# A hybrid two-layer backbone on one core: an earlier modulation vector, a rotation on VectorE, and a pinned VectorE order

## The chip, the cores and the metric

One core of a Trainium2 chip runs the whole program. The metric is the device time of one execution in microseconds (us); where several runs were made, their median.

## The reference

The program is a two-layer backbone over 512 latent tokens and 256 context tokens with a model width of 1024, all in fp32. Every sub-block reads a normalised and modulated copy of the stream, `rms(x) * (1 + scale) + shift`, and adds its result back times a gate. Shift, scale and gate are vectors of width 1024 per layer; there are six of them (modulations 0 to 5), each the product of a conditioning vector with a 1024 x 1024 block of a weight matrix, once for the latent and once for the context tokens.

- Layer 0: a convolution module and a bidirectional mLSTM side by side; their outputs together (width 1024) go through an out-projection, times gate 2, into the stream. Then a convolutional feed-forward network (FFN).
- Layer 1: multi-head latent attention, 16 heads. Queries come from a 512-wide latent, keys and values from a 256-wide one. Each head has 64 plain and 32 rotary components; both are normalised over the 96 (QK-norm), and the rotary part is turned by a position-dependent angle, which is two products and a sum. The attended values go through an out-projection, times gate 2, into the stream. Then a second FFN.

```python
def _modulate(x, shift, scale):
    return _rms(x) * (1 + scale) + shift
```

## The kernel before, in words

The stream lies in SBUF as eight tiles `xr`, one for each block of 128 features (index m or k), 128 partitions by 768 tokens: latent first (`LSEG`), then context (`CSEG`); `HSEG` are the two latent halves of 256 tokens. A product in fp32 is made of three matmuls, high by high, low by high and high by low part. `weights` (L158) brings a weight tile: a DMA on SP's queue into `wr`, a rounding copy `wh` on ScalarE (L113), and the difference `wl` on the engine that `lo_eng` names (L167), VectorE or, in some stages, GpSimd (POOL). `residual` adds gate times projection to the stream on VectorE (`xr<-pab,mods,xr`, or `pmo` in the attention, L119); `sumsq` squares the new stream tile on ScalarE (`sq`) and adds it into `ss` on POOL or VectorE (L253), after k; `norm_rows` sums `ss` over partitions on TensorE (`pr`) and takes the reciprocal root in eleven small VectorE instructions (`ra`, `rs`, then three rounds of `rz`, `rz`, `rs`; L199 ff.); `pb` spreads the result over the partitions by TensorE; then `u`, `fh`, `fl` make the modulated stream in two parts.

A scheduler orders the instructions of each engine by priority and by when they become ready in its own model; each engine then runs its list in order. Three places matter here.

- **Out-projection of layer 0** (`mixer0`, L533, its last loop over m, L716 ff.; 400 to 465 us). For each of the first six m, 48 matmuls `pab` over 768 tokens; m = 6 and 7 go by segment. A background generator `ada_gemv` (L335) makes modulation 5 meanwhile, in two halves of 512 columns. A half is eight loads `gr` (256 KB each on SP's queue, two buffers) with two VectorE instructions each that add row block times conditioning value into the accumulators `ga` (one for latent, one for context); `ada_sum` (L357) then folds the partitions by eight pairs of small matmuls `pac<-selv,ga` on TensorE, called the fold-in below, and VectorE puts the result into `mods`. At the end of each m, `self.step(AOS)` (L724) runs AOS steps of the generator; AOS is a constant at L44.
- **First queries of the attention** (`mixer1`, call at L1227; `prep_q`, L1286). After the queries' reciprocal root `rq`, the engine given as last argument scales the query tile `qt` (128 x 1536, L1301) and rotates its rotary part with eight smaller instructions (L1309 to L1312). Around it VectorE copies the low parts of the values `v`, makes a `wl`, and runs the keys' chain: `ssk`, `ra`, `rk`, `rz` ..., and `kt` (L1362, L1363), which TensorE's transposes `ptr` (L1378) wait for.
- **Last attention projection** (`project(3)`, L1446). All eight m for the first latent half, then for the second; before m = 4 of the second (`NRM`), the norm of the first half is issued (`norm_rows(HSEG[0])`). The FFN that follows begins with that norm's `pb`.

Of the kernel before, what the change touches and what calls it, by code (L numbers as in the profile page):

```python
# [19 lines left out]
LAT = 512  # L20
CTX = 256
T = LAT + CTX
# [7 lines left out]
HSEG = ((0, LAT // 2, 0), (LAT // 2, LAT, 0))  # L30
# [10 lines left out]
GRID_W = 64  # L41
NEG = -1.0e30
WPRIO = 300
AOS = 5  # L44
SLB = 6
PADB = 6
TAP = 8
# [33 lines left out]
class Net:  # L81
# [97 lines left out]
    def proj_tok(self, ps, wt, w0, wn, xs, t, nk, first=True, last=True, k0=0):  # L179
        wh, wl = wt  # L180
        for k in range(nk):
            xh, xl = xs[k0 + k]
            for j, (w, x) in enumerate(((wh, xh), (wl, xh), (wh, xl))):
                self.mm(ps, x[:, t * P:(t + 1) * P], w[:, k, w0:w0 + wn],
                        first and k == 0 and j == 0, last and k == nk - 1 and j == 2)

    def ahead(self, gen, prio):

        while True:
            with self.tc.high_priority(offset=prio):  # L190
                if next(gen, self) is self:
                    return
            yield
# [339 lines left out]
    def mixer0(self, pes):  # L533
# [3 lines left out]
        with ExitStack() as es:  # L537
# [178 lines left out]
            for m in range(KD - KDL):  # L716
# [5 lines left out]
                for seg in both:  # L722
                    self.sumsq(xs[m], m, seg, ob, "sq", bufs=2)
                self.step(AOS)  # L724
            ws = {m: self.weights(wout, 0, KD, m * P, P) for m in range(KD - KDL, KD)}
# [426 lines left out]
    def mixer1(self, xs):  # L1152
        nc, tc, d = self.nc, self.tc, self.d
        win = d["mla_w_in"][0]
        wuq, wukv, wout = d["mla_w_uq"][0], d["mla_w_ukv"][0], d["mla_w_out"][0]
        with ExitStack() as es:
# [8 lines left out]
            with ExitStack() as hes:  # L1165
# [5 lines left out]
                def tmp(s):  # L1171
                    return tp.tile([P, T], F32, tag="t", name=self.name(s))
# [52 lines left out]
                    nc.vector.tensor_scalar(kvt[t][:, :256], kvt[t][:, :256], rk[:, t:t + 1], None, op0=ALU.mult)  # L1225
                qt0 = self.query_tile(ap)
                for _ in self.prep_q(0, qt0, cqs, tb, wuq, lambda: tmp("sq")[:, :4 * QK].rearrange("p (h c) -> p h c", c=QK),  # L1227
                                     [xs[k][:, LAT:T] for k in (2, 3)], nc.gpsimd):
                    pass
                for k in range(2):  # L1230
                    ps = self.psum("pkvT")
# [82 lines left out]
    def attention(self, es, ap, qt0, xs, cqs, kvs, krr, ssr, tb, wuq, wukv, wout):  # L1314
        nc, tc = self.nc, self.tc
        tk = es.enter_context(tc.tile_pool(name="tk", bufs=1))
        qts, kts, vts, heads, prob, pts, outs, ohl, sums = {}, {}, {}, {}, {}, {}, {}, {}, {}
# [97 lines left out]
        def values(i):  # L1415
            h, u = divmod(i, 2)
            pr, hh = divmod(h, 2)
            pt = pts.pop(i)
            v = vts[pr]
            pv = self.pt("T", "ppv")  # L1420
            for j in range(NT):
                for p, x in enumerate(pt[j // 2]):
                    self.mm(pv[:, :256], v[:, j, hh, :], x[:, j % 2, :], j == 0 and p == 0, j == NT - 1 and p == 1)
            o = xs[4 + (2 * pr + u) % 4][:, LAT:T]
            outs[pr, u] = o
            own = slice(64 * hh, 64 * hh + 64)
            oth = slice(64 - 64 * hh, 128 - 64 * hh)
            tmp = xs[i % 2][:, LAT:T]
            self.act(tmp[own], pv[oth, :256])
            self.tt(o[own], pv[own, :256], tmp[own], ALU.add)  # L1430
            if i % 4 == 3:
                oh = tk.tile([P, LAT], F32R, tag="oh", bufs=2, name=self.name("oh"))
                ol = tk.tile([P, LAT], F32R, tag="ol", bufs=2, name=self.name("ol"))
                r = share.pop(pr)
                ps = self.pt("T", "pshr")
                for t in range(NTL):
                    self.mm(ps[:, t * P:(t + 1) * P], self.sel_two(t), r, True, True)
                for u in range(2):
                    c = slice(u * 256, (u + 1) * 256)
                    self.tt(outs[pr, u], outs[pr, u], ps[:, c], ALU.mult)  # L1440
                    self.split(outs[pr, u], oh[:, c], ol[:, c])
                ohl[pr] = (oh, ol)
                if pr % 2:
                    self.bg.append(project(pr // 2))

        def project(g):  # L1446
            ins = [ohl[2 * g], ohl[2 * g + 1]]
            if g == 3:
                ws = [self.weights(wout, 2 * g, 2, m * P, 512) for m in (0, 4)]
                for seg in HSEG:  # L1450
                    for m in range(KD):
                        if seg is HSEG[1] and m == NRM:
                            self.norm_rows(HSEG[0])
                        ps = self.pt("T", "pmo")
                        self.proj(ps, ws[m // 4], (m % 4) * P, ins, 2, (seg,))
                        self.residual(xs[m], ps, 1, 2, m, (seg,))
                        self.sumsq(xs[m], m, seg, tk, "pe", bufs=4)
                    yield
                return
            for m in range(0, KD, 4):  # L1460
                w = self.weights(wout, 2 * g, 2, m * P, 512)
                for i in range(4):
                    ps = self.pt("T", "pmo")
                    self.proj(ps, w, i * P, ins, 2, (LSEG,))
                    self.residual(xs[m + i], ps, 1, 2, m + i, (LSEG,))
                    yield
# [119 lines left out]
```

## Time and profile before

| | |
|---|---|
| time, median of 3 runs | 1783.05 us (1782.91, 1783.05, 1785.39) |
| profiled execution, its time | 1782.59 us |
| span of its trace | 1780.8 us |
| mean granted TensorE clock | 0.96 of full |
| busy: TensorE (PE), weight loads | 94 %, 85 % |
| busy: VectorE (DVE), ScalarE (ACT), POOL | 63 %, 38 %, 14 % |
| DMA | 95 GB/s mean |

A `timeline` row gives start, duration, engine, line, operation, output<-inputs by name, shapes, how many instructions the row joins (x), and in brackets the idle time ahead of it with what ended that. TensorE's own rows of a chain are matmuls at line 110. A granted clock of 1.00 stands for 2.4 GHz and 0.50 for 1.2 GHz.

### The profile page before, as it was taken

To read this page: it belongs to the slowest core of one execution; us is meant where nothing else is said; L and a number is where in the kernel's file an instruction comes from. 1 tells how busy PE (TensorE), PEld (TensorE's weight loads), DVE (VectorE), ACT (ScalarE), POOL (GpSimd) and SP (SyncE) were. 2 spreads that over 40 slices of the span, in tenths; PEclk is the share of its full clock that TensorE was granted. 3 is DMA by queue.
4 is the path that set the end of the run, shared out by engine and by line. 5 is a ranking of instruction groups with operands and counts; after the bars stand their busy time and mean duration, and the time that the engine had idled before them with its cause. 6 is when DMAs were issued, how large, how long until landed. Compare 5 with 4: busy or idle time off the path is not lost.

```text
span 1780.8 us, 24171 instructions
## 1 busy us (share of the span) xinstructions
PE 1679.1 (94%) x9436; PEld 1519.1 (85%) x9436; DVE 1130.3 (63%) x1743; ACT 679.2 (38%) x1364; POOL 246.0 (14%) x331
## 2 busy tenths in 40 slices
PE   6998698769999999999999998999999799999999
PEld 3998476659899999999999878999988788888887
DVE  3799964745876555474334487777788854444544
ACT  4421042542331221212222346777876442332232
POOL 2342132425100000000000111223140200000000
PEclk8999799779999999999999999999999899999999
DMA  9621442233253345262221332001110133333332
GB/s 311 216 61 42 135 143 83 61 118 100 74 159 106 108 142 166 84 200 67 64 60 49 97 96 61 32 13 36 44 35 25 36 95 97 101 98 95 95 95 83
DMA packets 194747, 168.43 MB, mean 95 GB/s; under 512 B 8552, under 2 KB 168214, under 8 KB 194632
## 3 DMA queue, kind: packets, MB, share of 16 engines
q1 hardware_dynamic: 191936, 163.30, 29.8%
q0 software_dynamic: 1280, 3.35, 0.8%
q8 instruction: 75, 1.23, 0.3%
q10 hardware_dynamic: 1416, 0.21, 0.1%
q14 instruction: 40, 0.33, 0.1%
HBM read 161.55 MB, written 5.29 MB: 94 GB/s over the span
## 4 chain that ended last, share of the span: by engine, by line
PE 81%; DVE 10%; DMA 3%; ACT 3%; issue 1%; POOL 1%; SPq 0%; ACTq 0%; DVEq 0%; POOLq 0%
PE pfo L110 17%; PE pfg L110 16%; PE pfv L110 16%; DVE acc L593 6%; PE psc L110 4%; PE pab L110 3%; PE ppv L110 2%; PE pt L1409 2%; PE po L110 2%; PE pf L110 2%; PE pmo L110 2%; PE puq L110 2%; PE pukv L110 2%; PE pv L110 1%; PE pn L110 1%
## 5 line engine op out<-in xcount | busy, mean ns | idle before, releaser
L113 ACT ACTIVATE wh<-wr 128x1024 fp32r<-128x1024 f32 (+3 forms) x205 | 204.4, 999 | 625.0 <-PE pfo L110 215.5
L167 DVE TENSOR_TENSOR wl<-wr,wh 128x1024 fp32r<-128x1024 f32 (+3 forms) x171 | 195.8, 1147 | 194.4 <-ACT wh L113 190.5
L110 PE MATMUL pfo<-hh,wh 128*128 128x384 f32 (+2 forms) x528 | 166.8, 355 | 0.0
L110 PE MATMUL pfo<-hl,wh 128*128 128x384 f32 (+2 forms) x528 | 166.6, 355 | 0.0
L110 PE MATMUL pfo<-hh,wl 128*128 128x384 f32 (+2 forms) x528 | 166.2, 354 | 0.0
L110 PE MATMUL pfg<-fh,wh 128*128 128x384 f32 (+1 forms) x504 | 152.0, 355 | 0.0
L110 PE MATMUL pfg<-fl,wh 128*128 128x384 f32 (+1 forms) x504 | 151.6, 354 | 0.0
L110 PE MATMUL pfg<-fh,wl 128*128 128x384 f32 (+1 forms) x504 | 151.2, 354 | 0.0
L110 PE MATMUL pfv<-fh,wl 128*128 128x384 f32 (+1 forms) x504 | 150.8, 353 | 0.0
L110 PE MATMUL pfv<-fl,wh 128*128 128x384 f32 (+1 forms) x504 | 150.8, 353 | 0.0
L110 PE MATMUL pfv<-fh,wh 128*128 128x384 f32 (+1 forms) x504 | 150.7, 353 | 0.0
L119 DVE SCALAR_TENSOR_TENSOR xr<-pfo,mods,xr 128x512 f32<-128x512 f32 (+1 forms) x128 | 83.7, 665 | 104.4 <-PE pfo L110 103.8
L593 DVE SCALAR_TENSOR_TENSOR acc<-up,par,acc 128x783 f32<-128x783 f32 x120 | 146.9, 1249 | 4.4 <-ACT acc L113 2.3
L167 POOL TENSOR_TENSOR wl<-wr,wh 128x1024 fp32r<-128x1024 f32 (+1 forms) x34 | 85.3, 2512 | 296.9 <-ACT wh L113 280.2
L253 POOL TENSOR_TENSOR ss<-ss,sq 128x256 f32<-128x256 f32 (+1 forms) x31 | 32.1, 1044 | 573.5 <-ACT sq L113 572.6
L119 DVE SCALAR_TENSOR_TENSOR ga<-gr,cc,ga 128x1024 f32<-128x1024 f32 (+1 forms) x84 | 96.0, 1161 | 22.6 <-DMA gr<-in_ada_w_dram 22.3
L110 PEld LDWEIGHTS pfo<-hl,wh 128*128 128x128 f32 x528 | 98.1, 189 | 8.9 <-issue 0.2
L110 PEld LDWEIGHTS pfo<-hh,wh 128*128 128x128 f32 x528 | 97.9, 189 | 9.0 <-ACT hh L113 0.4
L110 PEld LDWEIGHTS pfo<-hh,wl 128*128 128x128 f32 x528 | 97.9, 189 | 8.7
L116 DVE TENSOR_TENSOR ft<-ft,pfv 128x768 f32<-128x768 f32 (+1 forms) x42 | 34.4, 820 | 109.9 <-PE pfv L110 109.9
L110 PEld LDWEIGHTS pfg<-fh,wh 128*128 128x128 f32 x504 | 92.8, 189 | 6.5
L110 PEld LDWEIGHTS pfg<-fl,wh 128*128 128x128 f32 x504 | 92.8, 189 | 6.4
(418 smaller groups left out, 3711.0 us busy)
## 6 DMA issues: line engine op xcount, KB each, us to landing
wr<-in_ffn_w_in_dram SPq DMA_DIRECT2D x88, 512.0 KB, 4.0
gr<-in_ada_w_dram SPq DMA_DIRECT2D x48, 512.0 KB, 4.5
wa<-in_ada_w_dram SPq DMA_DIRECT2D x20, 1024.0 KB, 8.1
wr<-in_ffn_w_out_dram SPq DMA_DIRECT2D x32, 512.0 KB, 3.5
wr<-in_ab_w_in_dram SPq DMA_DIRECT2D x20, 512.0 KB, 5.2
wr<-in_ffn_w_out_dram SPq DMA_DIRECT2D x24, 384.0 KB, 3.3
gr<-in_ada_w_dram SPq DMA_DIRECT2D x16, 256.0 KB, 2.7
wr<-in_mla_w_out_dram SPq DMA_DIRECT2D x8, 512.0 KB, 3.4
```

What stands on the lines that cost most here:

```text
L110: self.nc.tensor.matmul(out, lhsT=lhsT, rhs=rhs, start=start, stop=stop)
L113: self.nc.scalar.activation(out, in_, func, **kw)
L116: self.nc.vector.tensor_tensor(out, a, b, op=op)
L119: self.nc.vector.scalar_tensor_tensor(out, a, s, b, op0=op0, op1=op1, **kw)
L167: self.lo_eng.tensor_tensor(lo[:, :n], raw[:, :n], hi[:, :n].bitcast(F32), op=ALU.subtract)
L253: eng.tensor_tensor(self.ss[:, s:e], self.ss[:, s:e], sq[:, s:e], op=ALU.add)
L593: nc.vector.scalar_tensor_tensor(acc[:, :CONVO], up[:, k:k + CONVO], self.convw[:, 4 * k + ct:4 * k + ct + 1], acc[:, :CONVO], op0=ALU.mul ...
L1409: nc.tensor.transpose(pt[:, o:o + P], pe[:, (j + jj) * P:(j + jj + 1) * P], self.ident)
```

## The change

Three edits. A: AOS is 9 instead of 5, so each m of the out-projection of layer 0 carries nine steps of the modulation generator. B: the first queries are scaled and rotated by VectorE instead of POOL. C: the VectorE instructions traced from the norm of the first half to the end of the second half's projection are tied to the order in which the program emits them.

```diff
@@ -41,7 +41,7 @@
-AOS = 5
+AOS = 9
@@ -183,6 +183,19 @@
+    def traced(self):
+        return self.nc.cur_bb.bb.instructions
+
+    def in_order(self, start, engine):
+
+        last = None
+        for i in list(self.traced())[start:]:
+            if i.engine == engine:
+                if last is not None:
+                    info = mybir.DependencyInfo(mybir.DependencyClass.NoSync, mybir.DependencyReason.DATA)
+                    self.tc.add_manual_dep(i, last.name, info, reason="norm ahead of the sums")
+                last = i
@@ -1225,7 +1238,7 @@
-                                     [xs[k][:, LAT:T] for k in (2, 3)], nc.gpsimd):
+                                     [xs[k][:, LAT:T] for k in (2, 3)], nc.vector):
@@ -1450,11 +1463,14 @@
                 for seg in HSEG:
                     for m in range(KD):
                         if seg is HSEG[1] and m == NRM:
+                            start = len(self.traced())
                             self.norm_rows(HSEG[0])
                         ps = self.pt("T", "pmo")
                         self.proj(ps, ws[m // 4], (m % 4) * P, ins, 2, (seg,))
                         self.residual(xs[m], ps, 1, 2, m, (seg,))
                         self.sumsq(xs[m], m, seg, tk, "pe", bufs=4)
+                    if seg is HSEG[1]:
+                        self.in_order(start, mybir.EngineType.DVE)
                     yield
```

What this moves in the engines' lists is shown at three places; the number behind a name tells tiles of one name apart.

A, TensorE's list at the end of the out-projection of layer 0, before: the second fold-in (`pac_3460`) stands behind the last projection matmul and ahead of the norm's `pb`.

```order
L110 MATMUL pab_3431<-hmh_2891,wh_3320 128x256
L110 MATMUL pab_3431<-hml_2893,wh_3320 128x256
L110 MATMUL pab_3431<-hmh_2891,wl_3321 128x256
L110 MATMUL pac_3460<-selv,ga_414_3153 128x2
L110 MATMUL pac_3460<-selv,ga_415_3154 128x2
L110 MATMUL pac_3460<-selv,ga_414_3153 128x2
L110 MATMUL pac_3460<-selv,ga_415_3154 128x2
```

The same list with the change, at the start of m = 5 (`pab_3266`; `pab_3193` is m = 4).

```order
L110 MATMUL pab_3193<-hmh_2891,wl_3189 128x384 x2
L110 MATMUL pab_3266<-uh_2440,wh_3261 128x384
L110 MATMUL pac_3250<-selv,ga_408_3090 128x2
L110 MATMUL pab_3266<-uh_2440,wh_3261 128x384
L110 MATMUL pab_3266<-ul_2441,wh_3261 128x384 x2
L110 MATMUL pab_3266<-uh_2440,wl_3262 128x384
L110 MATMUL pac_3250<-selv,ga_409_3091 128x2
L110 MATMUL pac_3250<-selv,ga_408_3090 128x2
```

The second fold-in has moved into the first matmuls of m = 5: its first matmul needs one accumulator (`ga_408`) complete and stands one projection matmul in, the next needs the other (`ga_409`). The first fold-in has moved one m earlier too, to the start of m = 3.

B, VectorE's list after the last `rq`, before.

```order
L119 SCALAR_TENSOR_TENSOR rq_8600<-rz_8602,rq_8600 128x16
L116 TENSOR_TENSOR v_8675<-pukv_8677,v_8675 128x4x64
L167 TENSOR_TENSOR wl_8915<-wr_8913,wh_8914 128x768
L116 TENSOR_TENSOR v_8675<-pukv_8698,v_8675 128x4x64
L116 TENSOR_TENSOR ssk_8676<-ssk_8676,ssr 128x12
```

With the change.

```order
L119 SCALAR_TENSOR_TENSOR rq_8600<-rz_8602,rq_8600 128x16
L1314 TENSOR_TENSOR qt_8518<-qt_8518,rq_8600 128x1536
L116 TENSOR_TENSOR v_8675<-pukv_8677,v_8675 128x4x64
L1322 TENSOR_TENSOR xr_2899<-qt_8518,sq 128x128
L167 TENSOR_TENSOR wl_8915<-wr_8913,wh_8914 128x768
L1322 TENSOR_TENSOR xr_2899<-qt_8518,sq 128x128
L1322 TENSOR_TENSOR xr_2901<-qt_8518,sq 128x128
L1324 TENSOR_TENSOR qt_8518<-qt_8518,cq 128x8x32
L1322 TENSOR_TENSOR xr_2901<-qt_8518,sq 128x128
L1325 TENSOR_TENSOR qt_8518<-qt_8518,xr_2899 128x8x32
L1324 TENSOR_TENSOR qt_8518<-qt_8518,cq 128x8x32
L116 TENSOR_TENSOR v_8675<-pukv_8698,v_8675 128x4x64
```

The nine instructions of the rotation now stand ahead of the keys' chain; one more of them and the third `v` copy follow before `ssk`.

C, VectorE's list from the second round of the norm on, before (`xr_2903` to `xr_2909` are m = 4 to 7 of the second half).

```order
L119 SCALAR_TENSOR_TENSOR xr_2905<-pmo_12697,mods_112,xr_2905 128x256
L116 TENSOR_TENSOR rz_12674<-rs_2023_12672 6x128
L119 SCALAR_TENSOR_TENSOR xr_2907<-pmo_12708,mods_112,xr_2907 128x256
L119 SCALAR_TENSOR_TENSOR rz_12674<-rz_12674,ra_12673 6x128
L119 SCALAR_TENSOR_TENSOR xr_2909<-pmo_12719,mods_112,xr_2909 128x256
L119 SCALAR_TENSOR_TENSOR rs_2023_12672<-rz_12674,rs_2023_12672 6x128
L116 TENSOR_TENSOR rz_12674<-rs_2023_12672 6x128
L119 SCALAR_TENSOR_TENSOR rz_12674<-rz_12674,ra_12673 6x128
L167 TENSOR_TENSOR wl_12972<-wr_12970,wh_12971 128x1024
L119 SCALAR_TENSOR_TENSOR rs_2023_12672<-rz_12674,rs_2023_12672 6x128
L253 TENSOR_TENSOR ss<-ss,sq_12727 128x256
L119 SCALAR_TENSOR_TENSOR u_12767<-xr_2895,mods_112,pb_12764 128x256
```

With the change, from the norm's last round on.

```order
L116 TENSOR_TENSOR rz_12674<-rs_2023_12672 6x128
L119 SCALAR_TENSOR_TENSOR rz_12674<-rz_12674,ra_12673 6x128
L119 SCALAR_TENSOR_TENSOR rs_2023_12672<-rz_12674,rs_2023_12672 6x128
L119 SCALAR_TENSOR_TENSOR xr_2903<-pmo_12686,mods_112,xr_2903 128x256
L119 SCALAR_TENSOR_TENSOR xr_2905<-pmo_12697,mods_112,xr_2905 128x256
L167 TENSOR_TENSOR wl_12972<-wr_12970,wh_12971 128x1024
L119 SCALAR_TENSOR_TENSOR xr_2907<-pmo_12708,mods_112,xr_2907 128x256
L119 SCALAR_TENSOR_TENSOR xr_2909<-pmo_12719,mods_112,xr_2909 128x256
L266 TENSOR_TENSOR ss<-ss,sq_12727 128x256
L119 SCALAR_TENSOR_TENSOR u_12767<-xr_2895,mods_112,pb_12764 128x256
```

The norm now runs without a residual in between; the four residuals, the `wl` and the last addition into `ss` (of k = 7) come between its end and the first `u`.

## Rows read from the trace of the kernel before

**Rows 1.** The page, chain of work that ended last, by engine.

```profile
PE 81%; DVE 10%; DMA 3%; ACT 3%; issue 1%; POOL 1%; SPq 0%; ACTq 0%; DVEq 0%; POOLq 0%
```

**Rows 2.** Windows: stretch, its length, busy PE, PEld, DVE, ACT, POOL, granted clock, DMA share, GB/s.

```profile
420.00:430.00 10.00, 10.00 (x65) 10.00 (x64) 6.62 (x8) 1.99 (x3) 4.69 (x3) 1.00 0.34 100
...
1116.00:1118.00 2.00, 2.00 (x9) 1.81 (x8) 1.76 (x5) 1.75 (x3) 0.00 (x0) 0.50 0.00 0
```

**Rows 3.** Timeline of TensorE, out-projection of layer 0.

```profile
421.14 1.84 PE L110 MATMUL pac<-selv,ga 128*128 128x2 f32 x16
422.84 0.60 PE L110 MATMUL pab<-uh,wh 128*128 128x384 f32 x2
...
431.32 0.52 PE L110 MATMUL pab<-uh,wh 128*128 128x384 f32 x2
...
457.83 1.84 PE L110 MATMUL pac<-selv,ga 128*128 128x2 f32 x16
461.06 1.15 PE L110 MATMUL pb<-rs,runs 6*128 6x128 f32 x8 [1.39 <-DVE mods L116]
```

**Rows 4.** Timeline of VectorE, the sixteen instructions of the second half.

```profile
423.10 3.12 DVE L347 TENSOR_SCALAR ga<-gr,cc 128x512 f32<-128x512 f32 x2
...
429.53 2.82 DVE L119 SCALAR_TENSOR_TENSOR ga<-gr,cc,ga 128x512 f32<-128x512 f32 x4 [1.50 <-DMA gr<-in_ada_w_dram]
432.26 1.14 DVE L119 SCALAR_TENSOR_TENSOR xr<-pab,mods,xr 128x512 f32<-128x512 f32 x2
433.70 5.07 DVE L119 SCALAR_TENSOR_TENSOR ga<-gr,cc,ga 128x512 f32<-128x512 f32 x4 [0.31 <-DMA gr<-in_ada_w_dram]
440.02 4.96 DVE L119 SCALAR_TENSOR_TENSOR ga<-gr,cc,ga 128x512 f32<-128x512 f32 x4 [1.25 <-DMA gr<-in_ada_w_dram]
```

**Rows 5.** Timeline of POOL, the same stretch.

```profile
432.32 2.40 POOL L167 TENSOR_TENSOR wl<-wr,wh 128x1024 fp32r<-128x1024 f32 x1 [5.50 <-ACT wh L113]
434.67 2.89 POOL L253 TENSOR_TENSOR ss<-ss,sq 128x512 f32<-128x512 f32 x2
```

**Rows 6.** Timeline of TensorE, attention's first transposes of the keys.

```profile
1113.90 1.49 PE L1378 MATMUL ptr<-ident,kt 128*96 128x128 f32 x6 [2.78 <-DVE kt L1363]
```

**Rows 7.** Timeline of VectorE, from the last `rq` to `kt`.

```profile
1103.23 0.43 DVE L116 TENSOR_TENSOR v<-pukv,v 128x256 fp32r<-128x256 f32 x1 [1.00 <-ACT v L113]
1104.44 1.52 DVE L167 TENSOR_TENSOR wl<-wr,wh 128x768 fp32r<-128x768 f32 x1 [0.79 <-ACT wh L113]
...
1110.09 0.58 DVE L119 SCALAR_TENSOR_TENSOR rz<-rz,ra 128x12 f32<-128x12 f32 x1
1110.71 0.17 DVE L119 SCALAR_TENSOR_TENSOR rk<-rz,rk 128x12 f32<-128x12 f32 x1
...
1112.22 0.96 DVE L1362 TENSOR_TENSOR kt<-kt,rk 128x768 f32<-128x768 f32 x1
1113.09 0.55 DVE L1363 TENSOR_TENSOR kt<-krr,rk 128x384 f32<-128x384 f32 x1
```

**Rows 8.** Timeline of POOL, first and last of the rotation's nine instructions.

```profile
1102.39 2.76 POOL L1301 TENSOR_TENSOR qt<-qt,rq 128x1536 f32<-128x1536 f32 x1 [65.86 <-DVE rq L119]
...
1109.90 0.74 POOL L1312 TENSOR_TENSOR qt<-qt,xr 128x256 f32<-128x256 f32 x1
```

**Rows 9.** Timeline of TensorE, first matmul of the FFN's norm.

```profile
1410.33 1.19 PE L110 MATMUL pb<-rs,runs 6*128 6x128 f32 x4 [6.30 <-DVE rs L119]
```

**Rows 10.** Timeline of VectorE, norm of the first half and what follows.

```profile
1402.82 2.06 DVE L119 SCALAR_TENSOR_TENSOR rz<-rz,ra 6x128 f32<-6x128 f32 x1
...
1409.91 0.27 DVE L119 SCALAR_TENSOR_TENSOR rs<-rz,rs 6x128 f32<-6x128 f32 x1
...
1411.56 0.48 DVE L119 SCALAR_TENSOR_TENSOR u<-xr,mods,pb 128x256 f32<-128x256 f32 x1 [1.04 <-PE pb L110]
...
1413.24 0.47 DVE L119 SCALAR_TENSOR_TENSOR fl<-u,mods,fh 128x256 fp32r<-128x256 f32 x1
```

**Rows 11.** Timeline of POOL, additions into `ss` of k = 4 to 6.

```profile
1405.93 2.47 POOL L253 TENSOR_TENSOR ss<-ss,sq 128x256 f32<-128x256 f32 x3 [0.46 <-ACT sq L113]
```

## The prediction
> **What bounds the kernel.** I read the page's chain first, then windows of the three places that the change touches, then the engines' timelines there. TensorE makes 81 % of the chain [rows 1], so an edit counts by what it does to TensorE's list: work added where TensorE is busy without a gap costs its full length, and work on another engine counts only where TensorE waits for it. The three places differ in this. In the out-projection of layer 0 TensorE has no gap: 10.00 us busy of 10.00 at a granted clock of 1.00 [rows 2]. Before the first attention transposes it waits 2.78 us for VectorE's `kt` [rows 6]. Before the last FFN it waits 6.30 us for VectorE's `rs` [rows 9].
>
> **Edit A, the modulation vector sooner.** Two fold-ins are moved by one m; their matmuls stay the same in number. One fold-in costs the dense stream 422.84 - 421.14 = 1.70 us [rows 3]. The first one was in the dense stream and stays in it: 0. The second stood after the last projection matmul, at 457.83, and there TensorE waited anyway: it idled another 1.39 us before `pb` at 461.06, the wait being put down to `mods` [rows 3]. Up to that `mods` VectorE was busy without a gap, with the norm and the last residual, and these stay; so taking fold-in and `mods` out of the tail gives back about one small VectorE instruction (0.17 [rows 7]), less overlap: I take 0.1 us. Nothing is the one end, the whole 1.39 the other. In m = 5 the same matmuls cost 1.70, since nothing covers them there.
>
> The larger question is whether `ga` is ready there. One m lasts 431.32 - 422.84 = 8.48 us [rows 3], and m = 5 begins at 431.32 in both versions, since one fold-in lies ahead of it in either. The new fold-in stands one projection matmul in: TensorE comes to it at 431.5. The chain of VectorE's sixteen instructions begins after the first fold-in, which comes one block earlier: 423.10 [rows 4] less 8.4 is 414.7. The first eight took from 423.10 to 432.35 [rows 4], 9.25 us with one wait for a load in it, and I let them take that again: 423.95. The other eight and the residual pair between them took from 432.35 to 444.98, 12.63 us [rows 4]: two waits for loads (0.31, 1.25) and instructions of 1.25 us each instead of 0.70, 2.82 / 4 in the quiet row [rows 4]. The slow ones lie beside POOL's `wl` (2.40) and its two additions (2.89) [rows 5], which occupy 5.3 of each 8.5 us. Quiet, they would take 8 x 0.70 + 1.14 = 6.7 us. In the new place they start later in POOL's cycle than before, so they meet it once rather than twice; I take 10.5 us, nearer to the 12.63 of the same loads than to the quiet sum. The accumulators are then complete at 434.5, and TensorE, which comes there at 431.5, waits **3.0 us**. The bounds: all sixteen quiet, 2 x 1.56 + 14 x 0.70 + 1.14 = 14.1, end at 428.8: no wait. At the whole old pace, 414.7 + 21.9 = 436.6: 5.1 us. SP's queue is passed by the same eight loads in another order: one of them now stands between the FFN's second and third weight load and none behind the third. That last `gr` waits if the weight load ahead of it waits for its buffer, which is a reason more not to take the quiet sum; the weight tiles themselves are for the FFN, which begins behind `pb` at 461 [rows 3], so 0 for them.
>
> Sum of A: 1.7 + 3.0 - 0.1 = **+4.6** (0.3 to 6.8).
>
> If TensorE could take the projection's matmuls that stand behind the fold-in first, the wait would be filled and A would cost 1.6. The trace speaks against it: in the 2.78 us before `ptr` [rows 6], a projection (`puq`) that stood behind in the list, with its operands ready, did not begin. The Trainium skill, page *TensorE: Matmul & The Clock Gate*, section "Step-by-step: what each phase is for", says the same: only weight loads are pulled ahead, matmuls stay in program order. By that rule the wait stands in full.
>
> **Edit B, the rotation on VectorE.** Added to VectorE: one instruction of 1536 elements, four of 128, four of 256. From `kt`'s two lengths, 0.96 for 768 and 0.55 for 384 [rows 7], 1.07 ns per element follow, so 1.78 for the first; 0.27 for each of the four short ones (a 128-element row [rows 10]); 0.43 for each of the 256 (`v` [rows 7]). That is 1.78 + 1.08 + 1.72 = 4.6, less nine times the 0.08 by which instructions overlap (1112.22 + 0.96 against 1113.09 [rows 7]): 3.9 us. Taken away: eight VectorE instructions between 1104.44 and 1110.09 ran long while POOL worked at the rotation from 1102.39 to 1110.64 [rows 8]. The first is `wl`, 1.52 against 0.96 for the same size; the last is `rz`, 0.58 against 0.17 [rows 7]; the eight excesses add up to 3.0. Filled: two waits for ScalarE, 1.00 and 0.79 [rows 7], 1.8 us. So `kt` ends 3.9 - 3.0 - 1.8 = **-0.9** earlier, and `ptr` behind it. The bounds: none of the excess comes back, 3.9 - 1.8 = +2.1; and the gain cannot pass TensorE's wait, -2.8. Behind the rotation wait the copies of `v`, which free the PSUM tiles of `pukv`; the first is about 0.8 us later, its matmuls have the wait at `kt` behind them, so 0.
>
> **Edit C, the pinned order.** Before, residuals stood between the norm's instructions, and `rs` ended at 1410.18 [rows 10]. Without the four residuals and the `wl` in between it ends near 1407.5, and `pb` can start 2.7 us earlier. But the work is only moved behind it: two residuals (to 1408.3), `wl` of 1.2 by the slope above (1409.5), two residuals (1410.2). POOL's additions of k = 4 to 6 (2.47 together [rows 11]) hang on those residuals, the last addition (k = 7) on POOL, and the first `u` stands behind that addition in VectorE's list. With the additions held until `wl` is through they end near 1411.7, the last addition at 1412.1; `pr`, four small matmuls like `pb`'s 1.19 [rows 9], takes 1.0, `ra` 0.3 [rows 10], and the first `fl` begins at 1413.4, where it was 1413.24 [rows 10]: **+0.2**. Bounds: the whole 2.7 gained; or additions, `wl` and `ss` all in a row, first `u` at 1412.4 instead of 1411.56 [rows 10]: +0.8.
>
> That the additions are held rests on one row: `rz` on 6 x 128 took 2.06 us while POOL's `wl` ran, against 0.27 for a like one [rows 10]. The Trainium skill, page *SBUF — State Buffer*, section "SBUF: two separate sides", has the rule: a VectorE instruction with two SBUF inputs and a GpSimd instruction share a port pair that the first holds to its end, and the other is blocked. By it C is +0.2; without it, the additions beside `wl` at 0.82 each, C would be -0.4.
>
> **The sum**: 4.6 - 0.9 + 0.2 = +3.9 us on the profiled execution's 1782.59: **1786.5**. The median of the three runs is 0.46 above that execution, which would make 1787.0 of it; I stay with 1786.5, since two of the larger unknowns (A's wait, the FFN's lead) can hardly go further up but well down. About 0.2 %, 3.6 us, is what a measurement can tell from no change: below 1779.5 is faster, above 1786.6 slower.
>
> **Rivals.**
> 1. *VectorE is ready before the fold-in.* All sixteen instructions are done by 431.5. For it: the quiet pace ends at 428.8. Against it: the loads, two buffers, kept the old chain waiting three times [rows 4]. Then A costs 1.6 and the sum is 1.6 - 0.9 + 0.2 = +0.9: 1783.5. Chance 0.25.
> 2. *The wait also lowers TensorE's clock.* After the wait of 2.78 us the granted clock was 0.50 in the next stretch [rows 2], 1.2 GHz, until about 1118: 4 us at half speed are 2 us lost. For A's wait of 3 us I price it at 2.5: 1789.0. Against it: the work ahead of that wait was dense, at `ptr` it was not. Chance 0.12.
> 3. *The rotation lengthens the keys' chain.* ScalarE, not VectorE, paces the stretch to `ssk`, so the blocked time isn't given back as a whole; `kt` comes 1.5 later in place of 0.9 earlier: 1788.9. For it: two waits were for ScalarE [rows 7]. It decides if `ssk` starts after 1108.8 (an estimate: without the excess some 4.8 us remain from there to the end of `kt`). Chance 0.10.
> 4. *Faster: the norm's lead reaches the FFN.* If the addition of k = 7 is done by the time `pb` is (1408.7), `u` starts there, and the 2.7 us of `rs` count in full; with rival 1's absence of a wait and B at -0.9 to -2.8 that is 1.6 - 0.9 - 2.7 = -2.0 to -3.9: 1780.6 to 1778.7. Against it: the addition stands behind four residuals and a `wl` on VectorE. Chance 0.10.
>
> That the change does not do what it says is excluded by the engines' lists: fold-in, rotation and norm stand where it puts them.
>
> **Numbers.** The forecast's own case has 0.43; it lies on the bound of 0.2 %, and half of it counts as same. Same: 0.21 + 0.25 (rival 1) + 0.02 = 0.48. Slower: 0.22 + rivals 2 and 3, less a little for an A below its bound, 0.42. Faster: 0.10, rival 4 and what I overlooked. The range: 1780.5 takes in rival 1 with B and C at half of their best ends, 1790.0 takes in rivals 2 and 3 with the 0.46 of the median.
>
> **What would show it.** A: a row of TensorE at the start of m = 5, `pac` with an idle time of 2 to 4 us released by VectorE's `ga`; no idle there is rival 1; a clock below 1.00 behind it is rival 2. In the tail, `pb` within 0.5 us of its old distance from the last `pab`. B: no POOL work between 1102 and 1111 (of before's time), `wl` back to about 1.0, and `ptr`'s idle time below 2.78. C: `rs` ends 2 to 3 us sooner, `pb` with it, but the first `fl` at its old distance from the last `pmo`; an `fl` two microseconds earlier refutes the term. The prediction is wrong if the stretch from 393 to 465 grows by under 1 us, or that from 1400 to 1415 shrinks by over 1.

## The result, and the profile after

Slower: 1797.07 us (median of 4 runs, 1795.10 to 1800.61) against 1783.22 for before (median of 4, 1782.91 to 1785.39). The ratio is 1.0077, its 95 % interval 1.0060 to 1.0095: about 14 us, where the forecast was 3.3 above this median of before and the top of its range 6.8 above it. The profiled execution took 1797.35 us, its span is 1795.3 us, 14.5 more than before's.

I divided the span at six TensorE rows that stand in both traces, and took the lengths of the pieces from their starts.

| piece | before, us | after, us | difference |
|---|---|---|---|
| start to the first `pab<-hmh` | 393.83 | 395.62 | +1.79 |
| out-projection of layer 0, to the FFN's `pb` | 67.23 | 78.54 | +11.31 |
| FFN of layer 0, to `pb` of the attention | 575.34 | 578.05 | +2.71 |
| to the first transposes of the keys | 77.50 | 76.45 | -1.05 |
| attention, to the last `pmo` after a wait | 279.25 | 277.69 | -1.56 |
| last projection, to the FFN's `pb` | 17.18 | 18.37 | +1.19 |
| last FFN, to the end | 370.47 | 370.58 | +0.11 |

The loss is in the out-projection, where edit A is. TensorE's timeline of after there; the fold-in rows answer to [rows 3].

```profile
414.59 1.84 PE L110 MATMUL pac<-selv,ga 128*128 128x2 f32 x16
...
433.17 0.34 PE L110 MATMUL pab<-uh,wh 128*128 128x384 f32 x1
438.46 0.56 PE L110 MATMUL pac<-selv,ga 128*128 128x2 f32 x2 [4.96 <-DVE ga L119]
438.88 0.67 PE L110 MATMUL pab<-uh,wh 128*128 128x384 f32 x1
439.35 0.84 PE L110 MATMUL pab<-ul,wh 128*128 128x384 f32 x2
...
440.31 2.98 PE L110 MATMUL pac<-selv,ga 128*128 128x2 f32 x14
...
474.16 1.16 PE L110 MATMUL pb<-rs,runs 6*128 6x128 f32 x8 [2.98 <-DVE xr L119]
```

Two things are to be seen. TensorE comes to the second fold-in after one matmul of m = 5 and waits 4.96 us for `ga`. And behind the wait everything is slow: two `pab` take 0.84 instead of 0.52, fourteen `pac` 2.98. The windows of after give the clock (columns as in [rows 2]):

```profile
414.00:424.00 10.00, 10.00 (x65) 10.00 (x64) 6.16 (x7) 2.00 (x3) 4.70 (x3) 1.00 0.36 105
434.00:438.40 4.40, 0.00 (x0) 0.00 (x0) 3.92 (x4) 0.61 (x1) 3.77 (x2) 0.92 0.31 96
438.40:442.00 3.60, 3.54 (x15) 3.57 (x15) 1.64 (x3) 0.94 (x2) 1.57 (x2) 0.50 0.50 146
442.00:446.00 4.00, 4.00 (x16) 4.00 (x16) 0.17 (x1) 0.00 (x0) 0.38 (x1) 0.50 0.00 0
446.00:450.00 4.00, 4.00 (x20) 4.00 (x19) 0.00 (x0) 0.00 (x0) 0.00 (x0) 0.76 0.00 0
```

Full speed ahead of the wait, 0.50 (1.2 GHz) for the whole of 438.4 to 446, and 1.00 again only within the last row. Over 430 to 450 the mean is 0.74, so about 0.26 x 2 x 20 = 10 us were at half speed, and half of that, 5 us, is lost.

VectorE's timeline of after, the sixteen instructions; it answers to [rows 4].

```profile
416.55 3.13 DVE L360 TENSOR_SCALAR ga<-gr,cc 128x512 f32<-128x512 f32 x2
419.60 1.89 DVE L119 SCALAR_TENSOR_TENSOR ga<-gr,cc,ga 128x512 f32<-128x512 f32 x2
424.23 2.74 DVE L119 SCALAR_TENSOR_TENSOR ga<-gr,cc,ga 128x512 f32<-128x512 f32 x4 [2.74 <-DMA gr<-in_ada_w_dram]
428.36 2.42 DVE L119 SCALAR_TENSOR_TENSOR ga<-gr,cc,ga 128x512 f32<-128x512 f32 x2 [1.39 <-DMA gr<-in_ada_w_dram]
...
431.36 1.40 DVE L119 SCALAR_TENSOR_TENSOR ga<-gr,cc,ga 128x512 f32<-128x512 f32 x2
...
433.67 1.91 DVE L119 SCALAR_TENSOR_TENSOR ga<-gr,cc,ga 128x512 f32<-128x512 f32 x2 [0.52 <-DMA gr<-in_ada_w_dram]
436.05 2.93 DVE L119 SCALAR_TENSOR_TENSOR ga<-gr,cc,ga 128x512 f32<-128x512 f32 x2 [0.48 <-DMA gr<-in_ada_w_dram]
```

They last from 416.55 to 438.98, 22.4 us; before it was 21.9. The first eight took 10.4 of it (9.25 worked out), the rest 12.0 (10.5 worked out, 12.63 before). The waits for loads are 2.74 + 1.39 + 0.52 + 0.48 = 5.1 us, more than the 3.1 of before. With the prediction's quiet sum of 14.1 that leaves some 3.2 us (an estimate) for instructions that ran long. Two of the last pairs took 2.42 and 2.93 instead of 1.40, and POOL was at work beside each; its rows answer to [rows 5]:

```profile
427.16 2.40 POOL L167 TENSOR_TENSOR wl<-wr,wh 128x1024 fp32r<-128x1024 f32 x1 [6.89 <-ACT wh L113]
432.23 2.80 POOL L266 TENSOR_TENSOR ss<-ss,sq 128x512 f32<-128x512 f32 x2 [2.66 <-ACT sq L113]
434.99 2.78 POOL L167 TENSOR_TENSOR wl<-wr,wh 128x1024 fp32r<-128x1024 f32 x1
```

SP's queue of after shows the last load going out behind an FFN weight load:

```profile
419.70 11.42 SPq L356 DMA_DIRECT2D gr<-in_ada_w_dram  x5
431.22 0.39 SPq L165 DMA_DIRECT2D wr<-in_ffn_w_in_dram  x1
432.78 0.33 SPq L356 DMA_DIRECT2D gr<-in_ada_w_dram  x1
```

Edit B, TensorE and VectorE of after; they answer to [rows 6, 7].

```profile
1128.66 0.83 PE L1391 MATMUL ptr<-ident,kt 128*96 128x128 f32 x6 [3.17 <-ACT v L113]
```

```profile
1118.13 1.76 DVE L1314 TENSOR_TENSOR qt<-qt,rq 128x1536 f32<-128x1536 f32 x1
...
1120.34 0.95 DVE L167 TENSOR_TENSOR wl<-wr,wh 128x768 fp32r<-128x768 f32 x1
...
1125.67 0.17 DVE L116 TENSOR_TENSOR rz<-rk 128x12 f32<-128x12 f32 x1
...
1127.85 0.55 DVE L1376 TENSOR_TENSOR kt<-krr,rk 128x384 f32<-128x384 f32 x1
```

The long product takes 1.76 (1.78 were estimated), `wl` is back to 0.95, the small steps to 0.17. `ptr` now has a longer wait, since the transposes of the queries no longer cut it in pieces, and the profile puts it down to ScalarE's copy of `v`, which ends as the row begins. `kt` ends only 0.26 ahead of the row, the same distance as before, so `kt` may still be what it waits for.

Edit C, TensorE and VectorE of after; they answer to [rows 9, 10].

```profile
1424.72 1.19 PE L110 MATMUL pb<-rs,runs 6*128 6x128 f32 x4 [6.22 <-DVE xr L119]
```

```profile
1421.59 0.28 DVE L119 SCALAR_TENSOR_TENSOR rs<-rz,rs 6x128 f32<-6x128 f32 x1
...
1422.59 1.20 DVE L167 TENSOR_TENSOR wl<-wr,wh 128x1024 fp32r<-128x1024 f32 x1
1423.72 0.86 DVE L119 SCALAR_TENSOR_TENSOR xr<-pmo,mods,xr 128x256 f32<-128x256 f32 x2
```

`rs` ends at 1421.87, but `pb` begins 2.85 later: it is released by the last residual, at 1424.58.

### The profile page after: what moved, and what is told of

Same layout as the page of the kernel before. It is cut to its first block, busy times and chain, and to the rows that moved or that the text cites. A ratio compares the mean times of both kernels' runs of the same rounds, so it can differ in the third digit from the quotient of the medians.

```text
span 1795.3 us, 24169 instructions
## 1 busy us (share of the span) xinstructions
PE 1691.7 (94%) x9436; PEld 1528.1 (85%) x9436; DVE 1129.2 (63%) x1752; ACT 679.8 (38%) x1364; POOL 241.0 (13%) x322
## 4 chain that ended last, share of the span: by engine, by line
PE 81%; DVE 11%; DMA 3%; ACT 3%; issue 1%; POOL 1%; SPq 0%; POOLq 0%; DVEq 0%; ACTq 0%
PE pfo L110 17%; PE pfg L110 16%; PE pfv L110 16%; DVE acc L606 6%; PE psc L110 3%; PE pab L110 3%; PE ppv L110 2%; PE pt L1422 2%; PE pmo L110 2%; PE po L110 2%; PE puq L110 2%; PE pac L110 2%; PE pukv L110 2%; PE pf L110 1%; PE pv L110 1%; PE pn L110 1%
```

## The experiments

Where nothing else is said, an edit is made to before. The lengths are those of the pieces of the table above, as differences from before's trace; "total" is the ratio of the times with its 95 % interval, against runs of before on the same chip.

| run | out-proj. | FFN 0 | to `ptr` | attention | to `pb` | total |
|---|---|---|---|---|---|---|
| e1, A alone | +11.66 | +2.72 | +0.68 | -0.36 | +0.03 | 1.0076 (1.0060 to 1.0091) |
| e2, B alone | +0.12 | +0.09 | -1.16 | +0.63 | +0.04 | 0.9998 (0.9988 to 1.0007) |
| e3, C alone | +0.32 | +0.06 | -0.14 | +0.12 | +0.02 | 1.0004 (0.9995 to 1.0014) |
| e4, B and C | +0.09 | +0.11 | -1.24 | +0.56 | +0.01 | 0.9998 (0.9989 to 1.0007) |
| e5, A, 4 buffers | +1.78 | -1.77 | +0.28 | -0.11 | +0.04 | 1.0026 (1.0016 to 1.0035) |
| e6, A, fold-in later | +1.76 | -0.41 | +0.38 | -0.60 | +1.18 | 1.0003 (0.9994 to 1.0013) |
| e8, AOS 8 | +0.07 | +0.03 | -0.07 | +0.05 | +0.03 | 0.9998 (0.9988 to 1.0009) |
| e9, A, no POOL `wl` | +8.70 | +2.64 | +0.36 | -0.34 | +0.04 | 1.0045 (1.0032 to 1.0057) |
| e10, A later, B, C | +1.90 | -0.56 | -0.85 | +1.25 | +1.24 | 0.9997 (0.9987 to 1.0007) |
| e12, A later, B | +1.76 | -0.39 | -0.88 | -0.48 | +0.03 | 0.9994 (0.9984 to 1.0005) |
| e11, A, 7 blocks | +6.17 | -1.86 | +0.57 | -0.26 | +0.02 | 1.0034 (1.0024 to 1.0044) |
| e13, A, 6 blocks | +1.43 | +1.46 | +0.23 | -0.01 | +0.01 | 1.0013 (1.0002 to 1.0025) |
| e14, C, `wl` behind | +0.33 | +0.03 | -0.13 | +0.16 | -1.21 | 0.9995 (0.9985 to 1.0006) |
| e15, e14 and B | +0.07 | +0.08 | -1.16 | +0.53 | -1.21 | 1.0000 (0.9991 to 1.0009) |
| e16, A, fold-in of two | +8.34 | -0.49 | +0.08 | -0.32 | +0.01 | 1.0040 (1.0025 to 1.0054) |

The first piece, ahead of all three edits, varies from 393.5 to 396.4 without a relation to them (e5 excepted, below), so the +1.79 there is not the change's.

**The parts apart.** Each part alone, and B with C.

```diff
-AOS = 5
+AOS = 9            # e1
-  [xs[k][:, LAT:T] for k in (2, 3)], nc.gpsimd):
+  [xs[k][:, LAT:T] for k in (2, 3)], nc.vector):    # e2, e4
+  self.in_order(start, mybir.EngineType.DVE)        # e3, e4
```

> Edit A alone (AOS 9), the rest as before. Theory 1 (the accumulators of the second half come late, TensorE waits some 5 us with nothing else to do, and its clock falls behind the wait): pac at the start of m = 5 with an idle time of 4.5 to 5.5 us released by ga, granted clock 0.50 for about 9 us behind it, the stretch up to the FFN's first pb longer by 10 to 12 us, total +10 to +14. Rival 2 (the loss is spread: clock phases in the first 130 us and in the FFN, which any reordering shifts): the stretch longer by 6 or less, and shifts of 1 to 2 us elsewhere also without A.

> Edit B alone (first queries rotated by VectorE). Theory 1: kt sooner by about 1 us and, since the transposes of the queries no longer wait for POOL, no clock drop behind the wait at ptr: -2 to -3.5 in total, granted clock 1.00 in the 4 us behind ptr. Rival 2 (the clock there depends on what came before in the program, not on B): only -0.5 to -1.2, clock 0.50 behind ptr as before.

> Edit C alone (norm pinned ahead of the residuals). Theory 1 (pb waits for the last residual, which frees the PSUM tile that pb's pool takes over, so an earlier rs gains nothing and the later residual costs): pb released by VectorE's xr, about 1.2 us later than before, total +1 to +1.5. Rival 2 (pb's release by xr is a by-product of A and B): pb sooner than before by 1 to 2.7 us, total -1 to -2.5.

> The change without edit A (AOS back to 5). Theory 1: the sum of B and C, -2.5 to 0 against before, so that A carries 11 to 16 us of the loss. Rival 2: +2 to +5, if the shifts in the first 130 us (+1.7) and in the FFN of layer 0 (+2.7) have nothing to do with A.

A alone has the whole loss, at the same two pieces and with the same wait of 4.96; theory 1 holds, and B and C together are no different from before. B does what was worked out up to `ptr` (-1.16), but half comes back in the attention, at a low clock behind the wait as in before: its rival 2. C moves nothing at all, less than either theory said; its `pb` was released by `xr` as theory 1 has it, yet no later (what became of the prediction's steps in it is shown at Edit C below):

```profile
1413.08 1.19 PE L110 MATMUL pb<-rs,runs 6*128 6x128 f32 x4 [6.31 <-DVE xr L119]
```

The +1.19 in after's last projection is thus not C's. It is in e6, which has no C, too: there the clock fell behind the wait of 1.66 at the first `pmo`, where it stayed up in before.

**What makes the accumulators late.** A with four load buffers; A with `wl` made by VectorE; AOS 8, which issues a half's loads as close together, but leaves the fold-ins where they were.

```diff
-  raw = alloc("gr", 2)[:, :wide]
+  raw = alloc("gr", 4 if layer == 0 else 2)[:, :wide]   # e5
+  self.lo_eng = nc.vector       # e9, ahead of the loop over m
-AOS = 5
+AOS = 8                         # e8
```

> Edit A alone, with four load buffers instead of two for the modulation generator of layer 0. Theory 1a (the loads make the accumulators late: VectorE waited 2.74 + 1.39 + 0.52 + 0.48 = 5.1 us for them in the changed kernel): VectorE's ga run through with under 1.5 us of waits for loads, TensorE's idle time at the second fold-in under 1 us, the clock stays at 1.00, the stretch up to the FFN's first pb is 1.5 to 3 us longer than before, total +1 to +4. Rival 1b (POOL's instructions make them late): the loads come, but the ga still end about 3 us or more after TensorE is there; total +8 or more.

> Edit A alone, with the out-projection's wl made by VectorE instead of POOL. Theory 1a (loads): the ga wait for loads as in the changed kernel, and TensorE's wait at the second fold-in stays at 4 to 6 us, since VectorE has 1.2 us more per m; total +11 to +15. Rival 1b (POOL holds VectorE up): the ga take 0.70 each throughout, the wait falls under 2 us, total +2 to +6.

> AOS 8 alone: the loads of a half are issued within one m as with 9, the fold-ins stay where they were before (start of m = 4, and the tail). Theory 1: the same time as before within 2 us, no wait at either fold-in. Rival 2 (eight loads in one m disturb the weight loads or VectorE's residuals): +3 or more, with waits of TensorE inside m = 4 or 5.

With four buffers the sixteen instructions take 15.4 us (420.39 to 435.84), there is one load wait of 0.32, and TensorE goes into the fold-in without idling:

```profile
436.66 0.52 PE L110 MATMUL pab<-hmh,wl 128*128 128x384 f32 x2
437.02 1.84 PE L110 MATMUL pac<-selv,ga 128*128 128x2 f32 x16
438.72 0.60 PE L110 MATMUL pab<-uh,wh 128*128 128x384 f32 x2
```

So taking the load waits away is enough to take the wait away, theory 1a: the chain is 7.0 us shorter, of which about 1.2 is the residuals, which the scheduler put behind the chain in this kernel. Its total is not a clean measure, because the larger pool moved the mLSTM's order and the first piece grew by 5.8 us.

Without POOL's `wl` the wait falls to 1.61, but not by a shorter chain: it took 22.2 us (416.85 to 439.08), with load waits of 2.88, 1.39 and 0.32, and VectorE now made two `wl` of 1.2 itself. What comes sooner is the first accumulator, 19.4 us behind the chain's start instead of 21.8: its last instruction took 0.89, where it took 2.27 beside POOL's `wl` in after. The second is as late as it was, and the scheduler put ten projection matmuls ahead of its part of the fold-in, and ten instead of one ahead of the whole:

```profile
436.40 0.35 PE L110 MATMUL pac<-selv,ga 128*128 128x2 f32 x2 [1.61 <-DVE ga L119]
...
439.14 3.15 PE L110 MATMUL pac<-selv,ga 128*128 128x2 f32 x14
```

So POOL has a part in the wait, but the lists moved with it, and its part alone is tested by no run. Neither expectation for e9 had the total, since the clock took 10 us at half speed here too. With AOS 8 nothing is lost: not the bunched loads, but the place of the second fold-in.

**The fold-in one block later.** One more empty step ahead of the second fold-in, for A alone, for the whole change, and for the change without C.

```diff
-  for _ in range(2):
+  for _ in range(3 if layer == 0 and mod == 5 and k1 else 2):
       yield True
```

> Edit A alone, with one more empty step ahead of the second fold-in, so that it stands at the start of m = 6, one block later. Theory 1 (the wait and the clock behind it are the loss; a fold-in in the dense stream without a wait costs only its matmuls): no idle time at the fold-in, clock 1.00, the stretch 1.5 to 2 us longer than before, total +1 to +4. Rival 2 (the fold-in's place outside the tail is what costs, since the tail is then empty and the FFN begins at the low clock): the stretch from the last projection matmul to 500 us still 2 us longer than before, total +5 or more.

> The whole change (A, B, C), but with the second fold-in one block later, at the start of m = 6, as in the run that did this to A alone. Theory 1: no wait and no clock loss in the out-projection, so the 11 us are gone; what is left is the fold-in's 1.7 in the dense stream and the small effects of B and C: -2 to +2 against before. Rival 2 (B and C add to A's loss in the whole change): +3 or more.

> The same without C: A with the later fold-in, and B. Theory 1: within 1 us of the run with C, since pb waits for the last residual either way; -2 to +2 against before. Rival 2: 1.5 us or more faster than the run with C.

No wait, clock 1.00, and the piece is 1.76 longer: the fold-in's own matmuls, as worked out (1.70). The 11 us are gone with it, in A alone as in the whole change. These kernels and before can't be told apart in time.

**What the clock's loss hangs on.** Fewer row blocks shorten the chain of `ga`; fewer fold-in matmuls leave the wait as it is. A fold-in of half a modulation is four pairs of matmuls (not eight, as the description of the kernel has it), and the trace gives each of them two records: sixteen records, which e16 cuts to four.

```diff
-  for k in range(KD):
+  for k in range(7 if layer == 0 else KD):    # e11; e13: 6
...
-  for k in range(n): ...                      # 16 records
+  self.mm(p2[:, :2 * n], a[:, :P], self.cc[:, :n]..., v == 0, v == len(accs) - 1)  # e16: 4
```

> Edit A alone, with seven of the eight row blocks of modulation 5 added (the last load and its two instructions left out, so that modulation 5 is incomplete). Theory 1 (the clock falls behind any wait here of a microsecond or more, by a fixed amount): the wait shrinks by one load's pace to 1.5 to 3 us, the clock is at 0.50 for the same 10 us as in the whole change, and the stretch up to pb is 8 to 10 us longer than before. Rival 3 (the clock's loss grows with the wait): the low time shrinks with the wait to 6 us or less, the stretch 5 to 7 us longer.

> The same with six of the eight row blocks (modulation 5 incomplete). Theory 1: no wait at the fold-in or under 0.5 us, clock 1.00 throughout, the stretch 1.5 to 2.5 us longer than before: the fold-in's own matmuls alone. Rival 3 (fold-ins of small matmuls lower the clock by themselves): the clock falls here too, and the stretch is 5 us or more longer.

> Edit A alone, with the sixteen small matmuls of the second fold-in cut to two (each accumulator's first block alone, so that half of modulation 5 is wrong); its place and its wait for the accumulators stay. Theory 1a (the wait alone lowers the clock): the wait is 4.5 to 5.5 us, the low time behind it about 10 us as in the whole change, the stretch 9 to 10.5 us longer than before. Rival 1c (the fold-in's small matmuls at the low clock hold it there): the wait is the same, the low time 3.5 us or 7 us, the stretch 6 to 8.5 us longer.

The window from 430 to 450 of e9 (wait 1.61, sixteen records in the fold-in), e11 (wait 1.27 + 0.69, sixteen), e16 (wait 4.96, four) and e13 (no wait, sixteen), in this order; the clock is the third number from the end.

```profile
430.00:450.00 20.00, 18.39 (x84) 17.68 (x83) 9.37 (x13) 2.69 (x5) 5.00 (x4) 0.74 0.25 76
```

```profile
430.00:450.00 20.00, 18.05 (x93) 16.88 (x93) 5.82 (x10) 4.86 (x8) 10.83 (x7) 0.91 0.23 66
```

```profile
430.00:450.00 20.00, 15.04 (x71) 14.57 (x71) 9.02 (x13) 3.99 (x6) 7.52 (x5) 0.83 0.26 79
```

```profile
430.00:450.00 20.00, 20.00 (x113) 18.81 (x112) 6.48 (x12) 4.82 (x8) 11.05 (x8) 1.00 0.27 78
```

The time at half speed is some 10, 3.5, 7 and 0 us, so 5, 1.8, 3.4 and 0 are lost. e16 keeps the wait and loses 3.4: that is the wait's own. The whole fold-in behind the same wait makes it 5: the small matmuls that run at half speed keep the clock down longer, the rival 1c. It agrees that in e11 the records ran ahead of the fall of the clock, fourteen of them in 1.72 us, where e9's fourteen took 3.15 behind it:

```profile
433.02 0.35 PE L110 MATMUL pac<-selv,ga 128*128 128x2 f32 x2 [1.27 <-DVE ga L119]
434.06 1.72 PE L110 MATMUL pac<-selv,ga 128*128 128x2 f32 x14 [0.69 <-DVE ga L119]
```

So the low time goes with the small records that ran at half speed: 16 (after, e1) and 14 (e9) with some 10 us, 4 (e16) with 7, none (e11) with 3.5. e13 shows that a fold-in in the dense stream without a wait doesn't lower the clock. The loss does not go by the wait's length, though: e11's theory 1, a fixed amount, is not borne out by its 3.5 us, and rival 3, an amount that grows with the wait, not by e9, which loses three times as much behind a shorter wait. Each of these is one profiled execution, however, and e11's (1786.56 us) was 4.6 faster than the median of its eight times, 1791.18; so the low time may differ from execution to execution of one kernel. Only the 10 us behind the wait of 4.96 stand in two traces, after and e1. With these the pieces add up: e16 4.96 + 3.4 = 8.4 (8.34 measured); e9 1.76 + 1.61 + 5.2 = 8.6 (8.70); e11 1.76 + 1.96 + 1.8 = 5.5 (6.17); A alone 1.76 + 4.96 + 5.2 = 11.9 (11.66).

**What holds `pb` at the last FFN.** C, with the FFN's next three `wl` tied behind the last addition into `ss`; and the same with B.

```diff
+  self.pin_last, self.pins = last, 3          # at the end of in_order
...
+  if getattr(self, "pin_last", None) is not None:     # in weights, behind wl
+      self.tc.add_manual_dep(i, self.pin_last.name, info, reason="weights behind the sums")
```

> Edit C alone, and the FFN's first wl put behind the last addition into ss, so that VectorE makes the four residuals without it in between. Theory 1 (pb waits for the last residual, whose PSUM tile it follows): pb's idle time 6.3 falls to about 5.1, released by xr; the first fl 0.5 to 1.2 sooner; total -1.5 to 0. Rival 2 (pb waits for rs alone): pb's idle time falls by 2 or more.

> The same with edit B, without A: the version that the runs so far point to. Theory 1: -2 to 0 against before. Rival: no different from before within 0.5 us, since TensorE's clock takes back what the waits give.

TensorE of e14:

```profile
1411.35 1.22 PE L110 MATMUL pb<-rs,runs 6*128 6x128 f32 x4 [5.08 <-DVE xr L119]
1413.61 1.02 PE L110 MATMUL pr<-ss,sel 128*6 128x128 f32 x4 [1.04 <-DVE ss L273]
1416.01 0.80 PE L110 MATMUL pf<-fh,wh 128*128 128x256 f32 x2 [1.38 <-ACT fh L113]
```

`pb` comes 1.2 sooner, by the length of the `wl` and with the last residual: theory 1. What it gains comes back at once, in two new waits (1.04 for POOL's sums, 1.38 for `fh`, since `wl` now stands ahead of the first `u`): the first `fl`, expected 0.5 to 1.2 sooner, comes 0.5 later. e15 is the version that the runs pointed to, B and this without A, and it is no different from before either; so no version tried here beats before.

## Why the prediction was wrong, point by point

- **The fold-in's own cost in the dense stream**, 1.70, less 0.1 in the tail: right. e6, e5 and e13 show 1.76, 1.78 and 1.43 where there is no wait.
- **The wait at the second fold-in**, the step that failed first: I let the last eight instructions take 10.5 us where they had taken 12.63, on the argument that POOL would be met once rather than twice. They took 12.0 and met it twice, and the first eight took 10.4 instead of 9.25, with a load wait of 2.74 instead of 1.50. The chain took 22.4 us instead of 19.8; the wait was 4.96 instead of 3.0, close to the bound of 5.1 that the old pace gave. The trace of before had named the loads as what held that chain [rows 4], and I had noted that the last load waits behind a weight load; both spoke for the old pace, and the load waits are what e5 removes.
- **The clock behind the wait**, the larger step that failed: nothing in the sum, a rival with a chance of 0.12 and a price of 2.5. It came, and cost 5: the price was taken from the wait at `ptr`, where there is no fold-in behind it. My argument against it, that the work ahead of the wait was dense, did not hold: the granted clock was 1.00 there (414 to 424) and 0.50 behind the wait.
- **The FFN of layer 0**, +2.7: not in the text at all. From the FFN on the lists of A alone and of before are the same, and the extra time is clock. In before's window from 550 to 670 the mean clock is 0.97, in after's, which holds the same two fold-ins of 32 records, 0.94. That is 0.03 x 2 x 120 = 7 us more at half speed, by clocks rounded to hundredths, so some 3 us lost, which is the size of the term.
- **Edit B**: -0.9 worked out, -1.05 in after, -1.16 in e2. The excess of VectorE under POOL came back as the sum had it. After it the attention gave half of it back in e2; in after the clock stayed at 1.00 behind `ptr`, which gave another 1.56. In no other run was it as much (e2 +0.63, e4 +0.56, e10 +1.25, e12 -0.48), so this part is luck.
- **Edit C**: +0.2 worked out for the first `fl`; in e3 it begins 20.24 us behind the last `pmo` after a wait, where it was 20.09 before, so +0.15. Counted from that `pmo` as in before, `rs` ends at 1407.5, the fourth residual at 1410.2, POOL's additions at 1411.6, the last addition at 1412.1, and `fl` begins at 1413.4: each step stands. What failed lies beside that path: I had `pb` start with `rs`, 2.7 us sooner, but it waits for the last residual too, and that cost nothing (e3 +0.02 to `pb`, the last FFN +0.05). That the residual's PSUM tile is what holds it is argued from the releaser, not shown by a run of its own. POOL and VectorE of e3, behind the norm:

```profile
1411.28 3.06 POOL L266 TENSOR_TENSOR ss<-ss,sq 128x256 f32<-128x256 f32 x3 [3.07 <-ACT sq L113]
```

```profile
1414.37 0.42 DVE L266 TENSOR_TENSOR ss<-ss,sq 128x256 f32<-128x256 f32 x1 [1.44 <-POOL ss L266]
...
1416.12 0.46 DVE L119 SCALAR_TENSOR_TENSOR fl<-u,mods,fh 128x256 fp32r<-128x256 f32 x1
```

  That POOL's additions are held beside `wl` decided between +0.2 and -0.4, and it held: the three took 3.06 us in after and in e3 beside that `wl` and 2.32 in e14 without it. The Trainium skill, page *SBUF — State Buffer*, section "SBUF: two separate sides", states such a lock between a VectorE instruction with two SBUF inputs and a GpSimd instruction, and the trace agrees with its direction.
- **TensorE takes no later matmul first**: right; the 4.96 us stood in full with the other 47 projection matmuls of m = 5 behind the fold-in, as the Trainium skill, page *TensorE: Matmul & The Clock Gate*, section "Step-by-step: what each phase is for", has it.

Put together, the forecast's +4.6 for A in the out-projection was 11.3: 2.0 of the miss is the wait, 5 the clock. The FFN's 2.7 came on top.

## What to carry to other kernels

Work that is moved into a dense stretch of TensorE costs its length and, if its operands come late there, everything behind it waits: compare the time at which TensorE gets there with the pace that the producers had before, slow-downs included, and don't improve that pace without a row that shows why. A wait inside a dense stretch has to be priced with the clock behind it, which here cost as much as the wait. A step that is needed by one instruction sooner gains nothing as long as that instruction has a second releaser: look for the next-to-last one before moving it.

## What the runs showed of the hardware

- The clock's loss behind a wait did not go by the wait: 1.61 us cost 5 us, 1.96 cost 1.8, 4.96 cost 5 with a fold-in behind it and 3.4 with a quarter of its matmuls, one profiled execution each. It went with the small matmul records that ran behind the fall of the clock: 14 of 16 in the first case, none in the second, 16 and 4 in the last two.
- Small matmuls alone can take the clock down, too: in the FFN of layer 0 TensorE's row of 32 records of `pac` is followed by `pfo` at half speed without any idle time (the first rows below, from after). They do not always: in e5 (last rows) and e11 the same row left it at 1.00, as a fold-in of sixteen records did in e13 and others.

```profile
567.88 4.15 PE L110 MATMUL pac<-selv,ga 128*128 128x2 f32 x32
571.89 0.99 PE L110 MATMUL pfo<-hh,wh 128*128 128x384 f32 x2
572.67 0.84 PE L110 MATMUL pfo<-hl,wh 128*128 128x384 f32 x2
...
578.07 0.51 PE L110 MATMUL pfo<-hl,wh 128*128 128x384 f32 x2
```

```profile
562.59 3.63 PE L110 MATMUL pac<-selv,ga 128*128 128x2 f32 x32
566.08 0.60 PE L110 MATMUL pfo<-hh,wh 128*128 128x384 f32 x2
```

- How long it stays down depends on what came before, and that repeats: this FFN, the same instructions each time, took 575.3 to 575.5 us in the seven kernels whose out-projection was as long as before's within 0.4 us (before, e2, e3, e4, e8, e14, e15), 578.0 to 578.1 in the three whose fold-in ran at half speed behind the wait (after, e1, e9; in e9 all but two of its records), and 573.5 to 576.8 in the others. What sets it stays open.
